# Output projection of a hybrid decoder layer: six of eight pairs of token tiles by seven block products instead of eight

## The chip, the cores and the metric

The kernel runs on one core of a Trainium2 chip. The metric is the device time of one execution in microseconds (us). Before the change the median of three runs is 2264.36 us (2264.03 to 2264.9).

The core's engines run at the same time, each through its own list of instructions in order: TensorE (PE) for matmuls and transposes, VectorE (DVE), ScalarE (ACT) and GpSimd (POOL) for element-wise work, and SyncE (SP), which issues nearly all DMAs. An instruction waits on semaphores for what it needs; everything behind it on the same engine waits with it.

## The reference

One layer of a causal decoder over 2048 tokens of width 1024, in float32:

```python
nx = rmsnorm(h, attn_norm_g[l])
proj = jnp.einsum('bsd,dp->bsp', nx, w_in[l])
...
mixed = jnp.concatenate([o_a, o_b], axis=-1).astype(h.dtype)
h = h + jnp.einsum('bsm,md->bsd', mixed, w_out[l])

nm = rmsnorm(h, mlp_norm_g[l])
a = jnp.square(jax.nn.relu(jnp.einsum('bsd,df->bsf', nm, w_ff1[l])))
h = h + jnp.einsum('bsf,fd->bsd', a, w_ff2[l])
return rmsnorm(h, final_norm_g)
```

`o_a` is chunked gated linear attention, `o_b` dilated sliding-window attention. The change concerns the line with `w_out`, and what lies directly around it: the norm behind it and the start of the MLP's first product. `w_out` is 1024 x 1024, `w_ff1` is 1024 x 4096.

## The kernel before

**Precision.** A float32 product is made of three TensorE matmuls in the type fp32r. Each operand is split into a high part (a copy on ACT that rounds, L486) and a low part (the difference, on DVE, L487). `mm3` (L142 to L144) then issues high x high, low x high and high x low into the same PSUM bank.

**Stages.** The input projection comes first; then attention, in units that go through PE, DVE, ACT and POOL, until about 870 us; then the output projection (870 to 1070); then the MLP's first product, and its second.

**The output projection** is the loop at L1399 over 16 token tiles of 128 rows, in the order 0, 4, 1, 5, 2, 6, 3, 7, 8, 12, ... so that tile t and tile t + 4 follow each other. For one tile `mix_T` (L1262) loads 128 rows of the mixed heads (`mixD`, 512 KB) and of the input `x` (512 KB) into one tile `mx`, makes 8 transposes (L510) into two PSUM banks and splits them into `mT`. Then 2 halves of the output width x 8 chunks of the inner size x 3 = 48 matmuls go into two banks of tag "a"; `w_out` lies in eight tiles `wo`, loaded and split by `load_wo` (L1088) during the end of attention. DVE adds each bank to the row of x (L1416), and the row is stored to `hD`.

**The norm** of a tile is `norm_to_T` (L1225), one tile later: ACT squares the row with a sum (L181), ACT makes 1/sqrt by Ln and Exp (L175, L176), DVE multiplies the row out of place (L183), PE makes 8 transposes, ACT copies the two banks into the four 128x512 parts of the tile `bb` (L1232): two parts from tile t, two from t + 4. After the second tile DVE forms four sums (L1236 to L1239), one in `bb` and three in a tile `tb`, and seven transposed "token sums" are stored to `hTD` (L1241). These are the token-side operands of the MLP's seven products.

**The MLP's first product** works the same way as the change: 2 x 2 blocks, seven products j in the order 1, 2, 6, 5, 7, 3, 4 instead of eight. `product1` (L1339) issues one product (12 matmuls) and chains it in PSUM; `prep1` (L1289) makes the weight sums of a product two jobs ahead into `w1comb`; `load_w1` (L1281) loads raw weights; `reload` (L1245) loads one token sum from `hTD` into a tile `rb` (1 MB) and splits it into a pair of tiles `hb` in two steps of 128x1024. For the first half of the tokens, three of the seven reloads are issued at the tiles in RELOAD (positions 10, 11, 12), three ahead of the MLP's loop, which begins at L1576, and one in it; `load_w1(0)` and the first two `prep1` are at positions 12 and 13.

**Room.** SBUF tiles come from one pool "u" of 25 places; a new tile waits until the tile that had its place is done with. PSUM has 8 banks: 2 of tag "a", 3 of "c", 2 of "d", 1 of "o".

**Order.** The program is written in the order of the loops, and a scheduler then settles each engine's own order by its estimate of when things are ready; only what is pinned with `keep_in_program_order` stays as written.

Of the kernel before, what the change touches and what calls it, by code (L numbers as in the profile page):

```python
# [18 lines left out]
D = 1024  # L19
# [10 lines left out]
W1AT = 12  # L30
# [4 lines left out]
RELOAD = (10, 11, 12)  # L35
# [81 lines left out]
def emit(tc, a, stop=99):  # L117
# [968 lines left out]
    WO = []  # L1086

    def load_wo(n):  # L1088
        for c in range(len(WO), len(WO) + n):
            raw = slot("woraw")[:, :D]  # L1090
            w = view(slot("wo", FR), (2, D))
            SP.dma_start(raw, wo[:, c])
            A.activation(w[:, 0], raw, AF.Copy)
            V.tensor_tensor(w[:, 1], raw, w[:, 0].bitcast(F32), op=OP.subtract)
            WO.append(w)

# [124 lines left out]
    gM = slot("gs")[:, :D]  # L1221
    bb, tb = slot("bb"), slot("tb")
    rb, TF, TB = [slot("rb")], {}, {}

    def norm_to_T(src, dst, t):  # L1225

        normed(src, dst, gM)
        half, i = t // HT, t % 4
        b = [view(bb[:, 512 * q:], (4, 128)) for q in range(4)]
        k = t % HT // 4  # L1230
        for q, pv in enumerate(transposed(dst)):
            A.activation(b[2 * k + q], pv, AF.Copy)  # L1232
        if k == 0:
            return
        (b11, b21, b12, b22), (t2, t4, t3) = b, [view(tb[:, 512 * q:], (4, 128)) for q in range(3)]
        V.tensor_tensor(b12, b12, b11, op=OP.subtract)  # L1236
# [8 lines left out]
    def reload(j, half, t=None):  # L1245

        if t is None:
            t = rb[turns[0] % len(rb)]
            turns[0] += 1
        SP.dma_start(t[:, :2048], hTD[half, j - 1].rearrange("p c s -> p (c s)"))  # L1250

        def rest():
            if j not in TF:
                TF[j] = [slot(f"hb{j}", FR) for _ in range(2)]
                TB[j] = [view(v, (4, 512)) for v in TF[j]]
            for cs in (slice(0, 1024), slice(1024, 2048)):
                split(*[v[:, cs] for v in TF[j]], t[:, cs])
                yield

        return rest()  # L1260

    def mix_T(t):  # L1262
        u = view(slot("mx"), (2, D))
        to = D - 128 if t < 8 else D
        for cs in (slice(0, 512), slice(512, to)) if t in (0, 4) else (slice(0, to),):
            SP.dma_start(u[:, 0, cs], mixD[t * 128:t * 128 + 128, cs])
        if t not in tiles[:2]:
            SP.dma_start(u[:, 1], x2[t * 128:t * 128 + 128])
        m = view(slot("mT", FR), (2, CH, 128))
        for q, pv in enumerate(transposed(u[:, 0], outs[3, 0][:, t, 1:129] if t < 8 else None)):  # L1270
            split(*[m[:, i, 4 * q:4 * q + 4] for i in range(2)], pv)
        return u, m


# [119 lines left out]

    tiles = [8 * half + i + 4 * k for half in range(2) for i in range(4) for k in range(2)]
    nxt = mix_T(tiles[0])
    late = None
    back = []
    for at, t in enumerate(tiles):  # L1399
        u, m = nxt  # L1400
        if at + 1 < NT:
            nxt = mix_T(tiles[at + 1])
# [7 lines left out]
        for q in range(parts_):  # L1410
            for n in range(2):
# [3 lines left out]
                if q == parts_ - 1:  # L1415
                    V.tensor_tensor(h[:, cs], p[n], u[:, 1, cs], op=OP.add)  # L1416
# [288 lines left out]
```

## Time and profile before

| | |
|---|---|
| median of three runs | 2264.36 us |
| the profiled execution, its own time | 2268.81 us |
| its span on the core | 2266.9 us |
| mean granted TensorE clock | 0.995 |
| output projection, first to last of its matmuls | 869.8 to 1070 us |

The profiled execution is a single one, taken with the profiler on, and a little longer than the median of the runs; differences are formed against its own time.

How to read the lines: the page's first part has, for each engine, the busy time, its share of the span and the number of instructions. PEld is the load of weights into the array, which overlaps with PE. A line of a group is: source line, engine, operation, output tile <- input tiles, shapes, count, then busy time, mean ns of one, and the idle time of the engine just before these instructions with what ended it ("<-DVE pt L882": DVE's result `pt` of line 882). A timeline line is: start, duration, the same names, and in brackets the idle time before. A line of a DMA is: tiles, queue, kind, count, size, and the median us from issue to landing. `ps_a` and so on are PSUM banks by tag.

### The profile page before, as it was taken

Reading aid. Unit: us, or ns where it says so; the run is one execution under the profiler, and the core shown is the slowest. Engines: PE = TensorE matmul, PEld = TensorE weight load, DVE = VectorE, ACT = ScalarE, POOL = GpSimd, SP = SyncE. Lnnn points to the kernel's source line nnn. Section 1 sums busy time; section 2 is a strip of 40 time slices with the busy share of each in tenths; the row PEclk is TensorE's granted clock in tenths of the full one; section 3 lists DMA queues with packets and bytes.
Section 4 is the critical chain, followed back from the end, with each engine's and each line's share of the span. In section 5 each row is a group of like instructions: output and inputs, shape, how many; then the busy total and the mean of one; then the engine's idle time right before and its main releaser. Section 6 shows DMA issues by size and latency. Waiting matters only on the chain.

```text
span 2266.9 us, 35208 instructions
## 1 busy us (share of the span) xinstructions
PE 2239.0 (99%) x12508; PEld 1937.2 (85%) x12508; DVE 1635.2 (72%) x3092; ACT 1216.7 (54%) x2421; POOL 484.8 (21%) x455
## 2 busy tenths in 40 slices
PE   9999999999999999999999999999999999999998
PEld 8977998799999998888888887888888888888876
DVE  8787778766677686445877678767686696566768
ACT  6664446535777883324655557555555433333435
POOL 1210002015286673000000000000006322032462
PEclk9999999999999999999999999999999999999999
DMA  6457854776667973678645456454479997676775
GB/s 205 133 181 226 254 165 124 222 248 224 211 211 218 298 219 130 211 229 281 203 133 160 128 165 220 159 171 156 137 248 286 300 318 264 219 252 240 255 264 177
DMA packets 361440, 478.59 MB, mean 211 GB/s; under 512 B 19957, under 2 KB 269318, under 8 KB 350128
## 3 DMA queue, kind: packets, MB, share of 16 engines
q1 hardware_dynamic: 356766, 467.69, 63.3%
q0 software_dynamic: 4352, 8.39, 2.0%
q8 instruction: 98, 1.61, 0.3%
q14 instruction: 78, 0.64, 0.1%
q10 hardware_dynamic: 146, 0.27, 0.0%
HBM read 326.54 MB, written 154.44 MB: 212 GB/s over the span
## 4 chain that ended last, share of the span: by engine, by line
PE 90%; DVE 3%; issue 2%; DMA 2%; POOL 1%; ACT 1%; POOLq 0%; SPq 0%; ACTq 0%; DVEq 0%
PE ps_a L143 10%; PE ps_a L142 10%; PE ps_a L144 10%; PE ps_c L143 8%; PE ps_c L142 8%; PE ps_c L144 8%; PE ps_a L892 4%; PE ps_d L143 4%; PE ps_d L142 4%; PE ps_d L144 4%; PE ps_o L144 4%; PE ps_o L142 4%; PE ps_o L143 4%; PE ps_d L873 3%; PE ps_c L855 2%
## 5 line engine op out<-in xcount | busy, mean ns | idle before, releaser
L1499 POOL TENSOR_TENSOR bs<-bs,rb 128x1024 f32<-128x1024 f32 x60 | 182.2, 3045 | 1071.1 <-DMA actD<-ring 831.5
L486 ACT ACTIVATE cb<-bs 128x1024 fp32r<-128x1024 f32 x104 | 110.3, 1060 | 275.4 <-issue 127.5
L487 DVE TENSOR_TENSOR cb<-bs,cb 128x1024 fp32r<-128x1024 f32 x104 | 156.4, 1504 | 133.4 <-ACT cb L486 133.3
L487 DVE TENSOR_TENSOR w1comb<-w1raw,w1comb 128x512 fp32r<-128x512 f32 x224 | 153.4, 687 | 89.5 <-ACT w1comb L486 88.9
L864 ACT ACTIVATE pe<-pe,O 128x256 f32<-128x256 f32 (+1 forms) x384 | 158.0, 454 | 54.2 <-DVE O L863 51.8
L892 PE MATMUL ps_a<-v,pt 128*128 128x65 f32 x1200 | 180.2, 255 | 5.3 <-DVE pt L882 4.3
L892 PEld LDWEIGHTS ps_a<-v,pt 128*128 128x128 f32 x1200 | 175.2, 196 | 7.7 <-DVE pt L882 5.4
L486 ACT ACTIVATE w1comb<-w1raw 128x512 fp32r<-128x512 f32 x224 | 139.4, 626 | 76.6 <-PE ps_c L144 27.1
L873 PE MATMUL ps_d<-ident,pe 128*128 128x128 f32 x600 | 159.9, 282 | 0.0
L863 DVE CUSTOM_DVE_ANT_0 pe<-ps_c,nb 128x256 f32<-128x256 f32 (+1 forms) x384 | 126.7, 361 | 43.2 <-PE ps_d L873 16.8
L286 ACT ACTIVATE wcomb<-wraw 128x512 fp32r<-128x512 f32 (+2 forms) x119 | 90.0, 757 | 101.3 <-PE ps_a L143 35.2
L142 PE MATMUL ps_c<-hb,w1comb 128*128 128x512 f32 x336 | 130.8, 389 | 0.5 <-ACT xs L1370 0.5
L143 PE MATMUL ps_c<-hb,w1comb 128*128 128x512 f32 x336 | 130.7, 389 | 0.0
L487 DVE TENSOR_TENSOR ca<-ra,ca 128x1024 fp32r<-128x1024 f32 x84 | 123.8, 1475 | 9.5 <-ACT ca L486 9.5
L144 PE MATMUL ps_c<-hb,w1comb 128*128 128x512 f32 x336 | 130.5, 389 | 0.0
L144 PE MATMUL ps_c<-cb,ca 128*128 128x512 f32 x312 | 121.8, 391 | 0.0
L143 PE MATMUL ps_c<-cb,ca 128*128 128x512 f32 x312 | 121.7, 390 | 0.0
L142 PE MATMUL ps_c<-cb,ca 128*128 128x512 f32 x312 | 121.6, 390 | 0.0
L873 PEld LDWEIGHTS ps_d<-ident,pe 128*128 128x128 f32 x600 | 110.0, 188 | 0.5 <-ACT pe L864 0.2
L1361 ACT ACTIVATE acc<-acc 128x512 f32<-128x512 f32 x96 | 60.7, 632 | 90.5 <-DVE acc L1376 36.2
L351 POOL TENSOR_TENSOR acc<-acc,misc 128x264 f32<-128x264 f32 (+1 forms) x32 | 38.7, 1221 | 316.3 <-DMA wraw<-w_in 204.0
L142 PE MATMUL ps_a<-wo,mT 128*128 128x512 f32 x256 | 101.2, 395 | 0.0
(411 smaller groups left out, 7104.9 us busy)
## 6 DMA issues: line engine op xcount, KB each, us to landing
ra<-actD SPq DMA_DIRECT2D x52, 1024.0 KB, 7.6
actD<-ring SPq DMA_DIRECT2D x176, 256.0 KB, 2.8
rb<-w_ff SPq DMA_DIRECT2D x88, 512.0 KB, 7.1
bs<-w_ff SPq DMA_DIRECT2D x72, 512.0 KB, 5.3
w1raw<-w_ff SPq DMA_DIRECT2D x64, 512.0 KB, 4.2
k<-kD SPq DMA_DIRECT2D x16, 1024.0 KB, 7.7
wraw<-w_in SPq DMA_DIRECT2D x48, 256.0 KB, 3.3
cmb<-boD SPq DMA_DIRECT2D x16, 528.0 KB, 6.5
```

The source lines that it names most:

```text
L142: T.matmul(out, sh, mh, start=first, stop=False, **kw)
L143: T.matmul(out, sl, mh, start=False, stop=False, **kw)
L144: T.matmul(out, sh, ml, start=False, stop=last, **kw)
L286: A.activation(hi, src, AF.Copy, scale=sc)
L486: A.activation(hi, src, AF.Copy)
L487: V.tensor_tensor(lo, src, hi.bitcast(F32), op=OP.subtract)
L863: V.tensor_tensor_reduce(p, s, bias, scale=1.0, scalar=BIG, op0=OP.add, op1=OP.min, accum_out=nm)
L864: A.activation(p, p, AF.Exp, bias=nm, scale=-1.0)
L873: T.transpose(pb[:, i * 128:i * 128 + 128], src, ident)
L892: T.matmul(self.b.opsum[:, n % 4], self.pt[:, i * 128:i * 128 + 128], self.b.v[:, blk, cols], start=first, stop=last)
L1361: A.activation(v, v, AF.Relu)
L1499: (engines or ((G,), (V, V))[len(sums) - 1])[e].tensor_tensor(v, v, r, op=OP.add if op == "+" else OP.subtract)
```

## The change

**Block products.** A pair of token tiles (t, t + 4) is a matrix of 256 x 1024. Split into 2 x 2 blocks (a11, a12 of tile t, a21, a22 of tile t + 4; each 128 x 512) and with `w_out` in 2 x 2 blocks of 512 x 512, its product takes seven block products instead of eight, with sums of blocks on both sides. The pairs 0 and 1 are computed as before, 48 matmuls a tile. The pairs 2 to 7 take seven products of 4 chunks x 3 matmuls. Products 1, 2 and 5 open a bank ("a", "o", "d"); 6, 7 and 4 continue in the bank of product 1, and 3 in that of product 5. After each product DVE adds the bank as it then is to the quarter of the rows that needs it.

```diff
+    def product0(g):
+        p, j = g // 7, order[g % 7]
+        if j in (1, 2, 5):
+            held0[j] = ps({1: "a", 2: "o", 5: "d"}[j])
+        b = held0[{6: 1, 7: 1, 4: 1, 3: 5}.get(j, j)]
+        c = combs0[g % 6]
+        for k in range(4):
+            mm3(b, c[:, 0, k], c[:, 1, k], *wo_part(j, k), k == 0 and j in (1, 2, 5), k == 3, skip_group_check=True)
+        e, n = {1: (0, 0), 2: (0, 0), 6: (0, 1), 3: (0, 1), 5: (1, 1), 7: (1, 1), 4: (1, 0)}[j]
+        x = xhs[p][:, e, 512 * n:512 * n + 512]
+        V.tensor_tensor(x, b, x, op=OP.add)
+        if j in (3, 4):
+            row_done(p, j == 4)
```

**Token blocks.** `raw_block` copies a bank of four transposes into a tile `ar` on ACT (four per pair). `prep0` splits the block of a product, three products ahead, into one of six halves of `mcomb`, and forms four sums in place in `ar` on DVE.

```diff
+    def raw_block(p, e, q):
+
+        if p < 8:
+            if not raw0:
+                raw0.append(view(slot("ar"), (4, 4, 128)))
+            A.activation(raw0[0][:, 2 * e + q], mix_block(p, e, q, "c"), AF.Copy)
...
+        a11, a12, a21, a22 = [raw0[0][:, n] for n in range(4)]
+        j, c = order[g % 7], combs0[g % 6]
+        split(c[:, 0], c[:, 1], {1: a11, 2: a12, 6: a11, 5: a21, 7: a11, 3: a12, 4: a22}[j])
+        if j == 2:
+            V.tensor_tensor(a21, a21, a22, op=OP.add)
+            V.tensor_tensor(a11, a21, a11, op=OP.subtract)
+            V.tensor_tensor(a12, a12, a11, op=OP.subtract)
+        if j == 6:
+            V.tensor_tensor(a11, a22, a11, op=OP.subtract)
```

**Weights.** `load_wo` splits the upper four chunks of `w_out` in two pieces of 128x512 each, which lie in tiles `wb1`, `wb12`. `mix_wo(c)`, called once in each of the four plain tiles, loads two chunks again, forms four sums on POOL and splits them into `wb5`, `wb6`, `wb4`, `wb7`.

```diff
+    def mix_wo(c):
+
+        raw = slot("wtraw")
+        SP.dma_start(raw[:, :D], wo[:, c])
+        SP.dma_start(raw[:, D:2 * D], wo[:, c + 4])
+        b11, b12, b21, b22 = [raw[:, 512 * k:512 * k + 512] for k in range(4)]
+        for dst, x, y, j in ((b12, b12, b11, 5), (b22, b22, b12, 6), (b21, b21, b22, 4), (b11, b22, b11, 7)):
+            G.tensor_tensor(dst, x, y, op=OP.subtract)
+            split(*block_view(j, c), dst)
```

**The norm** is cut into `norm_row` and `norm_sums`, which stand in a list and are taken by `next_norm` after products 0, 1 and 5 of a pair (for the last pair in the MLP's loop). The row is multiplied in place, in the tile `xh` from which it is stored; the four sums are made in place in `bb`, from which the token sums are stored; `tb` is gone. All norm transposes use the banks of tag "c".

```diff
+        V.scalar_tensor_tensor(h, h, r, gM, op0=OP.mult, op1=OP.mult)
...
+        store_T(t, *(((1, 0), (2, 1)) if k == 0 else ((3, 3),)))
+
+    def norm_sums(t):
+
+        b11, b21, b12, b22 = hb4
         V.tensor_tensor(b12, b12, b11, op=OP.subtract)
-        V.tensor_tensor(t2, b22, b12, op=OP.subtract)
-        V.tensor_tensor(t4, b21, t2, op=OP.subtract)
-        V.tensor_tensor(t3, t2, b11, op=OP.subtract)
-        for j, v in ((1, b11), (2, b21), (5, b12), (6, t2), (3, b22), (4, t4), (7, t3)):
-            SP.dma_start(hTD[half, j - 1][:, :, i * 128:i * 128 + 128], v)
+        V.tensor_tensor(b22, b22, b12, op=OP.subtract)
+        V.tensor_tensor(b21, b21, b22, op=OP.subtract)
+        V.tensor_tensor(b11, b22, b11, op=OP.subtract)
+        store_T(t, (5, 2), (6, 3), (4, 1), (7, 0))
```

**The reload** of the first half's token sums takes the form that the second half's had: 14 pieces of 512 KB through two tiles `rb`, loaded from ten products before the MLP on and split in the last six products and the first ones of the MLP. A sum's tiles `hb` take the places of block weights that are done with.

```diff
+    def token_pieces(half, first):
+
+        parts_at = {}
+        for n in range(14):
+            parts_at.setdefault(first + 1 + n * 4 // 5, []).append(n)
...
+        def step(at):
+            if at == first - 3:
+                while len(rb) < 2:
+                    rb.append(slot("rb"))
+                for n in range(4):
+                    load(n)
+            for n in parts_at.get(at, ()):
...
+                split(*[v[:, cs] for v in TF[j]], piece(n))
+                load(n + 4)
```

**The loop** over the products of pairs 2 to 7 (`half0` is `token_pieces(0, -7)`):

```diff
+    for g in range(14, 56):
+        p, i = divmod(g, 7)
+        prep0(g + 3)
+        product0(g)
+        if i in (0, 1, 5):
+            next_norm()
+        if i == 2:
+            load_x(p + 1)
+            raw_block(p + 1, 0, 0)
+            raw_block(p + 1, 1, 0)
+        if i == 3:
+            raw_block(p + 1, 0, 1)
+        if i == 4:
+            raw_block(p + 1, 1, 1)
+            load_mix(p + 2)
+        half0(g - 56)
+        if g == 49:
             load_w1(0)
-        if at == W1AT + 1:
-            prep1(0)
-            prep1(1)
-        late = (h, u[:, 0], t)
+        if g >= 54:
+            prep1(g - 54)
```

More of the change, by code (lines that the diff above doesn't have):

```diff
@@ L29 @@
 SLOT = 2112
-W1AT = 12
 AHEAD, LAG = 3, 2
@@ L1243, in emit @@
-    turns = [0]
[L1245 to L1272, printed above, removed]
+    gs, bb = slot("gs"), slot("bb")
@@ L1393, in some_sums @@
                 sums1.pop(0)
[L1395 to L1402, printed above, removed]
+    order = (1, 2, 6, 5, 7, 3, 4)
+    combs0, raw0, held0 = [], [], {}
+    def raw_block(p, e, q):
+        if p < 8:
+            if not raw0:
+                raw0.append(view(slot("ar"), (4, 4, 128)))
+            A.activation(raw0[0][:, 2 * e + q], mix_block(p, e, q, "c"), AF.Copy)
@@ L1571, in mm2 @@
             n % 4 == 3 and c == 1, skip_group_check=True)
[L1573 to L1574 removed]
     load_w1(1)
[L1576 to L1582 removed]
+    for at in range(len(jobs1)):
         prep1(at + 2)
```

179 lines of the change are left out of this document (119 added, 60 removed).

## The prediction

> **What bounds the kernel now.** I read the page from its top: busy time by engine, then the chain that ended last.
>
> ```profile
> span 2266.9 us, 35208 instructions
> ...
> PE 2239.0 (99%) x12508; PEld 1937.2 (85%) x12508; DVE 1635.2 (72%) x3092; ACT 1216.7 (54%) x2421; POOL 484.8 (21%) x455
> ...
> PE 90%; DVE 3%; issue 2%; DMA 2%; POOL 1%; ACT 1%; POOLq 0%; SPq 0%; ACTq 0%; DVEq 0%
> ```
>
> TensorE is busy 99% of the span and is 90% of the chain. That is an average, so I next read the busy time by engine in the stretches around the output projection (columns: stretch, length, busy time and records of PE, PEld, DVE, ACT, POOL, granted clock, DMA share, GB/s).
>
> ```profile
> 860.00:870.00 10.00, 7.72 (x53) 7.72 (x54) 8.97 (x30) 4.95 (x14) 4.68 (x10) 0.66 0.35 120
> 870.00:920.00 50.00, 50.00 (x251) 41.88 (x250) 25.66 (x46) 11.13 (x26) 6.88 (x9) 1.00 0.42 137
> 920.00:1020.00 100.00, 100.00 (x505) 84.49 (x504) 42.86 (x58) 29.97 (x66) 0.00 (x0) 1.00 0.68 211
> 1020.00:1070.00 50.00, 50.00 (x251) 42.15 (x250) 29.37 (x38) 21.05 (x40) 0.00 (x0) 1.00 0.82 271
> 1070.00:1100.00 30.00, 30.00 (x141) 24.76 (x140) 25.16 (x38) 20.95 (x36) 0.00 (x0) 1.00 0.93 297
> ```
>
> From 870 to 1100 us PE has no idle time at full clock, while DVE is busy 43 to 59% up to 1070 and POOL is nearly free. There, a matmul removed is worth its whole issue interval, as long as what replaces it stays under PE's time. At 1070 to 1100 DVE is at 25.16 of 30: that hand-over to the MLP has little cover left, and 870 was preceded by a stall.
>
> **What is removed, and its price.** Groups of 920 to 1020, one row of the tile `wo` over the whole run, and a stretch of the MLP's matmuls alone:
>
> ```profile
> L142 PE MATMUL ps_a<-wo,mT 128*128 128x512 f32 x127 | 50.2, 395 | 0.0
> ...
> L510 PE MATMUL ps_d<-ident,mx 128*128 128x128 f32 x61 | 9.3, 273 | 0.0
> L510 PE MATMUL ps_c<-ident,mx 128*128 128x128 f32 x60 | 9.0, 272 | 0.0
> ...
> L181 ACT ACTIVATE mx<-mx 128x1024 f32<-128x1024 f32 x8 | 8.4, 1052 | 0.0
> ...
> L486 ACT ACTIVATE mT<-ps_c 128x512 fp32r<-128x512 f32 x8 | 4.8, 599 | 2.6 <-PE ps_c L510 2.6
> ...
> L486 ACT ACTIVATE hb<-rb 128x1024 fp32r<-128x1024 f32 x2 | 2.0, 1065 | 0.0
> ...
> L510 PE MATMUL ps_d<-ident,O 128*128 128x128 f32 x3 | 0.8, 273 | 0.0
> ...
> L142 PE MATMUL ps_a<-wo,mT x256: 387/389/487, 869.8 to 1069.7; 128*128 128x512 f32 x128
> ...
> 1150.00:1175.00 25.00, 25.00 (x112) 1.00 0.49 157
> ```
>
> A record lasts some 390 ns but matmuls overlap, so the price is the interval: 25.00/112 = 0.2232 us. Check: 3 x 127 such matmuls are 85.0 us of the 100, and the 61 + 60 + 3 transposes share the other 15, 0.12 us each. L142 has 256 records, a third of the projection's 768 matmuls. The new kernel keeps four tiles at 48 (192) and gives each of six pairs 7 products x 4 chunks x 3 = 84 where there were 96: 192 + 504 = 696. The 256 transposes stay. So 72 x 0.2232 = **16.1 us off PE**. This term is the surest: the new matmuls have the form of the old.
>
> **What is added off PE.** Prices for a 128x512 on DVE and a 128x1024 split, from the timeline of DVE in its densest stretch, and DVE's multiply for the norm:
>
> ```profile
> 1081.24 2.35 DVE L487 TENSOR_TENSOR hb<-rt,hb 128x1024 fp32r<-128x1024 f32 x2
> ...
> 1085.78 0.68 DVE L487 TENSOR_TENSOR w1comb<-w1raw,w1comb 128x512 fp32r<-128x512 f32 x1
> ...
> 1092.39 0.69 DVE L487 TENSOR_TENSOR w1comb<-w1raw,w1comb 128x512 fp32r<-128x512 f32 x1
> ...
> L183 DVE SCALAR_TENSOR_TENSOR mx<-mx,stats,gs 128x1024 f32<-128x1024 f32 x8 | 10.2, 1277 | 2.2 <-ACT stats L176 2.2
> ```
>
> Between the last two rows lie eleven steps, 6.61 us: 0.60 us each; a 1024-wide split is 1.15, the multiply 1.2. Per pair DVE has 7 adds, 7 splits, 4 token sums, 4 norm sums (22 x 0.60) and 2 multiplies: 15.6 us, against PE's 84 x 0.2232 + 32 x 0.12 = 22.6. So in the steady stage DVE is covered, with 7 us over. ACT's 4 raw copies, 7 splits and 4 transposed copies at 0.6 and 2 squares at 1.05 are 11.1. The block weights of the products are made during the four plain tiles: 16 subtracts of 1.29 on POOL, which has almost nothing to do from 870 on, and 16 x 0.6 us of splits on ACT and on DVE, which have 39 and 24 us free in the first 50; their eight loads of 512 KB meet a DMA share of 0.42. The work itself costs nothing then, hidden under PE's matmuls; were that cover gone, DVE's 24 more adds, 24 sums and 16 splits would cost 38 us. What can cost is order, in four places.
>
> *Attention's tail (before 870).* The eight weight splits become eight of 128x512 and four of 128x1024, in another order. What they cost there now:
>
> ```profile
> 858.03 0.28 PE L873 MATMUL ps_d<-ident,pe 128*128 128x128 f32 x1
> 862.28 0.69 PE L892 MATMUL ps_a<-v,pt 128*128 128x65 f32 x2 [3.97 <-DVE pt L882]
> ...
> 862.98 0.52 PE L892 MATMUL ps_a<-v,pt 128*128 128x65 f32 x2
> ...
> 867.43 0.33 PE L892 MATMUL ps_a<-v,pt 128*128 128x65 f32 x2
> ...
> L1094 DVE TENSOR_TENSOR wo<-woraw,wo x8: 1225/1626/2355, 811.0 to 856.1; 128x1024 fp32r<-128x1024 f32 x8
> L952 POOL TENSOR_TENSOR O<-O,cmb x28: 1273/1294/2269, 636.9 to 876.0; 128x512 f32<-128x512 f32 x28
> ```
>
> DVE's last split, started at 856.1, took part in making PE wait 3.97 us. The new order could remove this stall or make a second: -4 to +4 us. I take 0, since as many bytes are split in the same stretch.
> After that stall the same L892 pair lasted 0.52 us until about 867, and 0.33 from 867.43, so about 2.4 us more went to a slower PE. The Trainium skill, "TensorE: Matmul & The Clock Gate", Part 1, says that an idle window of about 3.4 us halves PE's clock; the trace agrees (3.97 us idle, granted clock 0.66 in that slice). By it a single stall of 3.4 us at the hand-over would cost 2.4 more and the sum would be 2258; by the row taken stall by stall, each below that length, nothing is added. The sum below uses the latter.
>
> *From plain tiles to products (about 920).* `mix_wo(3)` loads 2 x 512 KB through SP, then 4 POOL subtracts (1.29 each) and 4 splits. In the issue order, its load stands on SP behind the `hTD` stores of the second tile's norm, and ACT's raw copies for the third pair stand behind its third split.
>
> ```profile
> 900.48 0.69 DVE L1416 TENSOR_TENSOR mx<-ps_a,mx 128x512 f32<-128x512 f32 x1 [2.07 <-PE ps_a L144]
> ...
> 907.89 0.69 DVE L1236 TENSOR_TENSOR bb<-bb 128x512 f32<-128x512 f32 x1 [0.38 <-ACT bb L1232]
> ...
> 913.20 0.69 DVE L1416 TENSOR_TENSOR mx<-ps_a,mx 128x512 f32<-128x512 f32 x1 [0.69 <-PE ps_a L144]
> ...
> hD<-mx SPq DMA_DIRECT2D x16, 512.0 KB, 3.3
> hTD<-bb SPq DMA_DIRECT2D x32, 256.0 KB, 3.7
> mx<-x SPq DMA_DIRECT2D x13, 512.0 KB, 6.3
> hTD<-tb SPq DMA_DIRECT2D x24, 256.0 KB, 6.3
> ...
> rb<-hTD SPq DMA_DIRECT2D x4, 512.0 KB, 5.9
> ```
>
> A tile takes 12.7 us (900.48 to 913.20, the same add one tile on); four end at 869.8 + 50.8 = 920.6. The norm's copies are done by 907.9; a 512 KB load lands 6.3 later, about 914; three subtracts and a split end at 918.5; four raw copies at 0.6 and the first split on ACT and DVE end at 922.1 or so. PE waits about 2 us for it: **2**, bounds 0 (copies placed earlier) and 6 (one more landing).
>
> *Within the six pairs.* Two waits are new. The norm now multiplies in place, so it waits for the row's store (3.3 us); and `norm_sums` overwrites the tiles from which `hTD` is stored, with `tb` gone, so DVE's second subtract waits for a store that is issued only after ACT's copy: 3.7 to 6.3 us. Behind it on DVE stand bank adds and splits. Splits are made three products ahead (8 us), but a chained bank must be added to `xh` before PE writes it again, one product (12 matmuls, 2.7 us) later. The sums mostly stand where an add has just been done, and DVE has 7 us over per pair. Bounds 0 and 6 (1.2 for each of five hand-overs); I take **1.75**.
>
> *Into the MLP (about 1040 to 1085).* The first product's token sums are 14 splits of 128x1024. Before, their loads were spread from the eleventh tile on; now they start ten products before the MLP, and each sum waits for the weights whose place it takes. `load_w1(0)` is moved behind the last pair's first product, the last pair's norms into the MLP's loop, so DVE has them all in one stretch. I counted in the issue order from the end of the last pair's first product. PE has 133 matmuls and 24 transposes up to the MLP's product 3: 29.7 + 2.9 = 32.6 us. DVE must first issue 12 splits, 2 multiplies and 29 of 128x512: 13.8 + 2.4 + 17.4 = 33.6. Eight entries on, the last row's multiply is through at 40.1, and its transposes are PE's next after 24 more matmuls, at 38.0. So DVE is 1.0 and then 2.1 us behind, if it starts on time; it stands behind a wait for a store then, for which I take half of a row's 3.3 us. The two lags on one engine aren't added: 2.1 + 1.65 = **3.75**, bounds 1 (starts on time, one row hidden) and 8 (one load's 5.9 us in the open beside the 2.1).
>
> **Sum.** -16.1 + 0 + 2 + 1.75 + 3.75 = -8.6. The profiled execution took 2268.81 us (its span 2266.9 and 1.9 around it): 2260.2 for its like. The median of the runs, 2264.36, is 4.45 lower, so the forecast is 2255.8, say **2256**.
>
> **Rivals.**
> (a) *All of it hidden*: stalls under 4 us in all. For: DVE at 43% in 920 to 1020, 7 us over per pair. Against: 25.16 of 30 at the hand-over. About 2.5 us of stalls: 2250.8.
> (b) *Given back at the hand-overs*: all upper halves, 4 + 4 + 6.5 plus 1.6 before 870: 16.1 of stalls, 2264.4, no change. For: the DMA share of 0.82 and 0.93 from 1020 to 1100, which lengthens loads. Against: PE was busy without a gap from 1020 to 1100, with the same splits inside.
> (c) *Slower: a serial reload.* With two `rb` tiles, loads of pieces 5 to 14 wait for a split on DVE; then 5.9 us landing, 1.06 ACT, 1.15 DVE: 8.1 us round. If SP's queue (behind stores that wait for DVE) lets only one product's pieces be in flight, each of the last five sums costs 8.1 rather than a product's 2.7: 27 us, -16.1 + 27 = +10.9, with nothing else, 2275.3. It decides (over 0.2% slower) from 16.1 + 4.5 = 20.6 us, that is 6.8 us per sum. Against it: four pieces are in flight by construction, 4.05 us per sum, which costs 6.7.
> (d) *The change doesn't do what it says*: counts would show 768 matmuls; the code leaves no doubt, so no chance is given.
>
> **Chances.** 0.2% (4.5 us) is about what can be told from no change here. Forecast (stalls of 4 to 11.5 us, 2252 to 2260) 0.44; (a) 0.18; (b) 0.22; (c) 0.16. So faster 0.62, same 0.22, slower 0.16. Range 2248 (no stall, 2248.3) to 2268, which leaves out most of (c); the forecast's own range is 2252 to 2260.
>
> **What would show it.** In the changed profile: 232 records of each third of the projection's matmuls; PE idle of some 2 us near 920 put down to a split or a raw copy, small gaps put down to bank adds of `xh` in between, and 3 to 4 us just before and in the MLP's first round put down to `hb` or to the norm's multiply; DVE nearly full there. Wrong would be: a gap over 3.4 us followed by half clock, `hb` splits idle on `rb` loads each round (then c), or no gaps (then a).

## The result and the profile after

The changed kernel takes 2281.51 us (median of four runs, 2278.43 to 2283.72) where the kernel before takes 2264.63 on the same chip (four runs, 2264.03 to 2266.3). The ratio is 1.0072 with an interval of 1.0055 to 1.009: slower by 0.7%, where 2256 was forecast and the range ended at 2268. The profiled execution took 2281.68 us, 12.87 more than the one before.

The first lines of the page of the changed kernel: span, busy time by engine, and shares of the chain that ended last.

```profile
span 2279.8 us, 35292 instructions
...
PE 2231.8 (98%) x12436; PEld 1928.3 (85%) x12436; DVE 1694.4 (74%) x3172; ACT 1250.1 (55%) x2483; POOL 502.2 (22%) x471
...
PE 85%; DMA 5%; DVE 4%; issue 3%; ACT 2%; POOL 1%; SPq 0%; POOLq 0%; DVEq 0%; ACTq 0%
```

PE has 72 records fewer (12436 for 12508), as counted, but only 7.2 us less busy time where 72 x 0.2232 = 16.1 were to go; and its idle time (span less busy) rose from 27.9 to 48.0. To see where, the busy time of the changed kernel by stretches (columns as before: length, PE, PEld, DVE, ACT, POOL, granted clock, DMA share, GB/s): first the whole stretch from attention's end to the MLP, then the stretches that were shown of the kernel before, then every ten microseconds in which the clock was below 0.99.

```profile
780.00:1124.00 344.00, 318.13 (x1847) 274.68 (x1847) 262.12 (x529) 195.94 (x440) 92.21 (x116) 0.96 0.69 223
...
860.00:870.00 10.00, 9.96 (x70) 9.36 (x70) 9.30 (x30) 6.33 (x20) 5.12 (x11) 0.84 0.99 375
870.00:920.00 50.00, 46.02 (x214) 37.94 (x213) 35.82 (x48) 15.93 (x33) 24.18 (x20) 0.93 0.49 165
920.00:1020.00 100.00, 93.77 (x478) 78.23 (x477) 73.01 (x103) 48.90 (x97) 6.57 (x5) 0.97 0.68 214
1020.00:1070.00 50.00, 45.34 (x216) 36.60 (x216) 39.29 (x55) 29.18 (x53) 0.00 (x0) 1.00 0.73 227
1070.00:1100.00 30.00, 24.44 (x111) 19.61 (x110) 24.31 (x32) 17.59 (x31) 0.00 (x0) 0.89 0.86 271
...
820.00:830.00 10.00, 7.71 (x63) 7.31 (x62) 5.69 (x14) 5.96 (x16) 9.63 (x13) 0.96 0.84 255
830.00:840.00 10.00, 10.00 (x82) 9.78 (x82) 9.61 (x34) 8.57 (x26) 9.17 (x9) 0.87 0.38 144
880.00:890.00 10.00, 6.02 (x17) 4.45 (x16) 9.90 (x19) 3.01 (x6) 1.97 (x2) 0.69 0.18 47
890.00:900.00 10.00, 10.00 (x48) 8.27 (x47) 5.92 (x6) 3.07 (x8) 6.43 (x4) 0.97 0.43 138
920.00:930.00 10.00, 5.75 (x35) 4.61 (x33) 10.00 (x10) 3.50 (x6) 6.57 (x5) 0.91 0.22 63
930.00:940.00 10.00, 8.02 (x33) 6.65 (x34) 7.21 (x12) 7.34 (x15) 0.00 (x0) 0.75 0.75 223
1080.00:1090.00 10.00, 5.41 (x28) 4.21 (x27) 10.00 (x13) 4.96 (x7) 0.00 (x0) 0.93 0.76 217
1090.00:1100.00 10.00, 9.03 (x34) 7.03 (x35) 6.24 (x9) 6.36 (x14) 0.00 (x0) 0.73 0.83 251
```

The row of the same stretch before (its MLP stands 10 us earlier, so it ends at 1114):

```profile
780.00:1114.00 334.00, 328.06 (x1934) 285.93 (x1933) 206.53 (x453) 161.20 (x384) 70.88 (x100) 0.99 0.68 217
```

Beside the rows that the prediction shows, PE has lost 4.0 us from 870 to 920, 6.2 to 1020, 4.7 to 1070 and 5.6 to 1100, where it had lost none, and DVE is at 73 rather than 43 us in the hundred from 920 and full in 920 to 930 and 1080 to 1090.

So most of the 12.9 us arises between 780 and the MLP. Matched matmul by matmul, the changed kernel is even 1.5 us ahead shortly before 780 (PE's row L1052 of 776.27 before, now L1050, starts at 774.80), and 10.2 us behind in the MLP (the 5000th matmul from the end starts at 1114.9 before and at 1125.1 after): the stretch loses 11.7. It has 19.9 us more of idle time (25.9 for 5.9) and 9.9 less of busy time, of which 1.5 are matmuls of attention that had run before 780. So of the 16.1 us of matmuls that went only 8.4 show: the others took 7.7 longer, and the low clock of the slices agrees: with 860 to 870, (1 - clock) x 10 us adds up to 13.5 us, before the change to 3.4 (860 to 870 alone, at 0.66). Some of that fell where PE had nothing to do. The other 2.7 us appear far into the MLP; they were not followed.

The idle time is found in PE's timeline: all waits over 0.3 us from 780 to 1124 (start, duration, names, in brackets the wait and what ended it).

```profile
828.26 1.19 PE L890 MATMUL ps_a<-v,pt 128*128 128x65 f32 x8 [2.29 <-ACT pt L878]
...
858.95 0.44 PE L890 MATMUL ps_a<-v,pt 128*128 128x65 f32 x2 [3.10 <-ACT pt L878]
...
885.04 0.80 PE L140 MATMUL ps_a<-wb,mT 128*128 128x512 f32 x1 [3.98 <-DVE xh L1541]
...
926.83 0.55 PE L1336 MATMUL ps_c<-ident,mx 128*128 128x128 f32 x3 [2.22 <-ACT ar L1467]
...
931.98 1.12 PE L1266 MATMUL ps_c<-ident,xh 128*128 128x128 f32 x4 [4.01 <-ACT ar L1467]
...
1055.88 0.50 PE L141 MATMUL ps_d<-wb,mcomb 128*128 128x512 f32 x1 [1.72 <-DVE mcomb L485]
...
1062.52 0.47 PE L140 MATMUL ps_d<-wo,mcomb 128*128 128x512 f32 x1 [1.34 <-ACT stats L173]
...
1067.22 0.50 PE L140 MATMUL ps_a<-hb,w1comb 128*128 128x512 f32 x1 [1.49 <-ACT w1comb L484]
...
1090.76 0.80 PE L140 MATMUL ps_a<-hb,w1comb 128*128 128x512 f32 x1 [5.36 <-ACT xs L1434]
```

Nine waits, 25.5 us, in four places: attention's tail (5.4; before it was 5.0, of which 3.97 at 862.28), one at 885 in the plain tiles, which no step of the prediction had (4.0), the hand-over to the products (6.2) and the one to the MLP (9.9). Between 932 and 1055 there is none: the six pairs run as they should. Each place was followed back to its cause.

**885: POOL beside DVE.** PE waits for DVE's add of the bank, L1541, which starts at 884.31. What DVE and POOL did just before, and again around 920, each from its own timeline:

```profile
878.05 1.32 DVE L936 TENSOR_TENSOR gla<-gla,cmb 128x8 f32<-128x8 f32 x1
...
884.31 0.68 DVE L1541 TENSOR_TENSOR xh<-ps_a,xh 128x512 f32<-128x512 f32 x1
...
921.05 1.77 DVE L485 TENSOR_TENSOR wb<-wtraw,wb 128x512 fp32r<-128x512 f32 x1
922.74 1.77 DVE L1274 TENSOR_TENSOR bb<-bb 128x512 f32<-128x512 f32 x1
...
926.09 0.68 DVE L1541 TENSOR_TENSOR xh<-ps_a,xh 128x512 f32<-128x512 f32 x1
```

```profile
878.05 3.92 POOL L1118 TENSOR_TENSOR wtraw<-wtraw 128x512 f32<-128x512 f32 x3
...
913.99 6.06 POOL L1118 TENSOR_TENSOR wtraw<-wtraw 128x512 f32<-128x512 f32 x4 [14.32 <-DMA wtraw<-w_out]
920.62 6.68 POOL L1118 TENSOR_TENSOR wtraw<-wtraw 128x512 f32<-128x512 f32 x4 [0.58 <-DMA wtraw<-w_out]
```

While POOL subtracts, a DVE operation of eight elements per partition takes 1.32 us, as long as one of POOL's (3.92/3 = 1.31), and one of 512 takes 1.77 rather than 0.68, in step with POOL's 6.68/4 = 1.67. The eight-element ones come in a chain that ends attention, which takes 4.9 us here (877.14 to 882.02); the one of 879.41 took 0.17, in the gap between two of POOL's. The bank's add stands behind this chain, and behind three multiplies of attention (L948, 1.8 us). The add at 926.09, which reads one operand from PSUM, takes its usual 0.68 although POOL is still at work.

**927 and 932: late weights.** The last two groups of subtracts wait for their loads, 14.32 us in the first case. SyncE's timeline shows where the loads stood:

```profile
889.22 13.15 SPq L1488 DMA_DIRECT2D hD<-xh  x2
...
907.01 0.53 SPq L1114 DMA_DIRECT2D wtraw<-w_out  x1
...
914.75 0.60 SPq L1114 DMA_DIRECT2D wtraw<-w_out  x1
```

The queue stood from 889 to 902 at the row's store, which waits for DVE's last add of the tile; so the loads left at 907 and 914.75, the slowed subtracts ended only at 927.3, and ACT, which takes each split in order, reached the raw copies that PE waits for (L1467) at 926.19. The wait at 932 ends with the third of these copies: on ACT it stands behind the squares of a norm, and those wait for DVE's add of 929.58.

**1056 to 1091: DVE full.** DVE's timeline before the first of these waits and inside, then ACT's around the last:

```profile
1047.46 0.69 DVE L1274 TENSOR_TENSOR bb<-bb 128x512 f32<-128x512 f32 x1 [2.78 <-DMA hTD<-bb]
...
1058.16 0.68 DVE L1508 TENSOR_TENSOR xh<-ps_a,xh 128x512 f32<-128x512 f32 x1
```

```profile
1089.16 1.06 ACT L484 ACTIVATE hb<-rb 128x1024 fp32r<-128x1024 f32 x1 [2.41 <-DMA rb<-hTD]
1090.13 0.58 ACT L1434 ACTIVATE xs<-ps_a 128x512 f32<-128x512 f32 x1
```

DVE waits 2.78 us for the store of a token sum before it may overwrite it, and from 1047.5 to 1074 it isn't idle once. PE's last wait ends with ACT's copy of an MLP bank, which stands behind a split that waited 2.41 for its reload. That load was issued only at 1083.25, when DVE's split of 1082.01 had freed its place: a late DVE and a reload's round trip act together here.

### The profile page after: what moved, and what is told of

Read it like the earlier page. It is cut to its first block, busy times and chain, and to the rows that moved or that the text cites. A ratio compares the mean times of both kernels' runs of the same rounds, so it can differ in the third digit from the quotient of the medians.

```text
span 2279.8 us, 35292 instructions
## 1 busy us (share of the span) xinstructions
PE 2231.8 (98%) x12436; PEld 1928.3 (85%) x12436; DVE 1694.4 (74%) x3172; ACT 1250.1 (55%) x2483; POOL 502.2 (22%) x471
## 4 chain that ended last, share of the span: by engine, by line
PE 85%; DMA 5%; DVE 4%; issue 3%; ACT 2%; POOL 1%; SPq 0%; POOLq 0%; DVEq 0%; ACTq 0%
PE ps_a L141 8%; PE ps_a L140 8%; PE ps_a L142 8%; PE ps_c L141 8%; PE ps_c L142 8%; PE ps_c L140 8%; PE ps_a L890 4%; PE ps_d L141 4%; PE ps_d L140 4%; PE ps_d L142 4%; PE ps_o L142 4%; PE ps_o L141 4%; PE ps_o L140 4%; PE ps_d L871 3%; PE ps_c L853 2%
## 5 line engine op out<-in xcount | busy, mean ns | idle before, releaser
L485 DVE TENSOR_TENSOR cb<-bs,cb 128x1024 fp32r<-128x1024 f32 x104 | 162.5, 1563 | 137.3 <-ACT cb L484 137.2
L485 DVE TENSOR_TENSOR ca<-ra,ca 128x1024 fp32r<-128x1024 f32 x84 | 118.6, 1412 | 5.8 <-ACT ca L484 5.8
L142 PE MATMUL ps_a<-wcomb,tb 128*128 128x256 f32 (+1 forms) x344 | 97.7, 284 | 0.0
```

Source lines behind the costliest of these rows:

```text
L142: T.matmul(out, sh, ml, start=False, stop=last, **kw)
L485: V.tensor_tensor(lo, src, hi.bitcast(F32), op=OP.subtract)
```

## The experiments

Each kernel was timed against the kernel before on the same chip. In the last column: PE's waits over 0.3 us from 780 to 1130 us in its profiled execution.

| run | edit of the changed kernel | matmuls off | median us | ratio [interval] | PE's waits, us |
|---|---|---|---|---|---|
| (the kernel before) | - | 0 | 2264.63 | 1 | 5.4 |
| (the change) | none | 72 | 2281.51 | 1.0072 [1.0055, 1.009] | 25.5 |
| e1_sums_dve | weight sums on DVE | 72 | 2270.56 | 1.0012 [1.0002, 1.0022] | 17.3 |
| e2_last_plain | last pair plain | 60 | 2275.35 | 1.0038 [1.0026, 1.005] | 21.6 |
| e3_three_plain | three plain pairs ahead | 60 | 2275.77 | 1.0035 [1.0022, 1.0048] | 17.8 |
| e4_plain_both | e2 and e3 | 48 | 2271.04 | 1.0011 [1.0, 1.0022] | 16.4 |
| e5_last_plain_dve | e1, last pair plain, loads sooner | 60 | 2268.48 | 1.0003 [0.999, 1.0016] | 14.5 |
| e6_raw_early | e1, first raw copies sooner | 72 | 2265.24 | 0.9986 [0.9971, 1.0] | 14.6 |
| e7_fewer_sums | e1, eight token sums left out | 72 | 2271.71 | 1.002 [1.0005, 1.0035] | 18.8 |
| e8_all_three | e5 and e6 | 60 | 2270.24 | 1.0009 [0.9997, 1.0022] | 15.5 |
| f1_own_place | e6, token sums without the wait for stores | 72 | 2265.9 | 1.0 [0.9989, 1.0011] | 15.6 |
| f2_norm_apart | e6, norm out of place | 72 | 2276.84 | 1.0044 [1.003, 1.0057] | 21.3 |
| f3_raws_sooner | e6, each pair's raw copies a product sooner | 72 | 2265.23 | 0.9986 [0.9977, 0.9996] | 10.7 |
| f4_both | f1 and f3 | 72 | 2268.56 | 1.0004 [0.9996, 1.0013] | 16.0 |
| g1_no_low_halves | e6, 14 low halves left out | 72 | 2261.09 | 0.9975 [0.9965, 0.9984] | 10.7 |
| g2_raws_pool | raw copies sooner, sums on POOL | 72 | 2281.67 | 1.0065 [1.0047, 1.0083] | 20.0 |

### Weight sums on DVE (e1)

```diff
-            G.tensor_tensor(dst, x, y, op=OP.subtract)
+            V.tensor_tensor(dst, x, y, op=OP.subtract)
```

> The sixteen weight sums of mix_wo go from POOL to DVE, nothing else. Theory P (POOL's subtracts slow DVE where both run): the 4.0 us gap of PE at 885 us and the half clock behind it go, DVE's 128x8 operations there are back at about 0.2 us from 1.2, and the hand-over near 925 loses about 3 of its 6.2 us: about 2270 us. Theory Q (the loads of w_out stand on SP behind stores that wait, and ACT's raw copies behind their splits): DVE only gets 16 x 0.6 us more, the gaps at 925 stay near 6 us: 2278 to 2282.

Sixteen subtracts move to the engine that is busier, and the ratio falls by 0.6%, some 13.6 us. The grouped rows of DVE's eight-element operation at that line (ns min/median/max, first and last start): the change, e1, and the same operation before.

```profile
L936 DVE TENSOR_TENSOR gla<-gla,cmb x2: 1159/1242/1325, 878.0 to 879.6; 128x8 f32<-128x8 f32 x2
```

```profile
L936 DVE TENSOR_TENSOR gla<-gla,cmb x2: 160/166/173, 879.0 to 879.4; 128x8 f32<-128x8 f32 x2
```

```profile
L938 DVE TENSOR_TENSOR gla<-gla,cmb x2: 165/168/172, 877.8 to 878.2; 128x8 f32<-128x8 f32 x2
```

With POOL's subtracts gone the operation is back at 0.166 us, and the wait at 885 is gone. At the hand-over to the products 2.23 and 0.34 us of wait are left of 6.2; those into the MLP stay (1.74, 1.34, 1.45, 4.08). That POOL's subtracts slowed DVE is shown by these rows: the chain is through in 1.7 us rather than 4.9. The 13.6 us are the price of the whole edit: 8.2 of waits, and most of the rest clock, as the stretches at half clock between 780 and the MLP go from 27.3 to 17.1 us. A new order is part of it, too: the scheduler now has the bank's add (880.69) ahead of the three multiplies, so the 4.0 us at 885 are not POOL's alone. PE's timeline of e1 at the hand-over:

```profile
922.08 0.55 PE L1336 MATMUL ps_c<-ident,mx 128*128 128x128 f32 x3 [2.23 <-ACT ar L1467]
...
926.34 0.63 PE L142 MATMUL ps_a<-wb,mcomb 128*128 128x512 f32 x1
926.76 0.63 PE L140 MATMUL ps_a<-wb,mcomb 128*128 128x512 f32 x1
...
930.73 0.40 PE L142 MATMUL ps_o<-wo,mcomb 128*128 128x512 f32 x1
930.97 0.40 PE L140 MATMUL ps_o<-wo,mcomb 128*128 128x512 f32 x1
```

After waits of 2.23 and 0.34 us the matmuls start 0.42 us apart, and from about 930.5 on 0.24. The granted clock is 0.50 from 923.54 to 930.37. So half rate also follows a wait well below the 3.97 us of the kernel before.

### The pairs next to the hand-overs made plain (e2, e3, e4)

e2 computes the last pair with 96 matmuls instead of 84, so that its token blocks need no sums close to the MLP; e3 makes pairs 0 to 2 plain and spreads the weight sums over tiles 1 to 4; e4 does both. Weight sums stay on POOL.

```diff
-    for g in range(14, 56):
+    for g in range(14, 49):
...
+    for e in range(2):
+        m = nxt
...
+                mm3(b[n], m[c // 4][:, 0, c % 4], m[c // 4][:, 1, c % 4],
+                    *wo_part(((1, 12), (2, 3))[c // 4][n], c % 4), c == 0, c == CH - 1)
```

```diff
-    for at in range(4):
+    for at in range(6):
...
-        mix_wo(at)
+        for c in {1: [0], 2: [1], 3: [2], 4: [3]}.get(at, ()):
+            mix_wo(c)
...
-    for g in range(14, 56):
+    for g in range(21, 56):
```

> The last pair is computed plainly (12 more matmuls, 2.7 us), five pairs by seven products; its split tiles lie in the places of mcomb. Theory D (DVE is crowded and late where the last pair's products, the 14 reload splits and the MLP's first weights meet, and the reload's round trips follow from it): the gaps of 9.9 us from 1055 to 1091 and some 3 us of slow clock shrink to under 3: about 2271 us. Rival R (the round trip of the reload through two rb tiles sets it, whatever DVE has to do): the gaps stay, 2282 to 2284.

> Three pairs plain at the start (12 more matmuls, 2.7 us), and mix_wo(0) to mix_wo(3) at the second to fifth tile, away from attention's tail. If the stalls at 885 and 925 come from the place of mix_wo (P or Q, both): 6.5 and 9 us go, about 2269 us, with PE idle under 1.5 us between 870 and 960. If the hand-over costs its 6 us wherever it lies, since raw copies and first splits can't be made ahead: the gap stands near 945, and the time is about 2277.

> Both: pairs 0, 1, 2 and 7 plain, four pairs by seven products, 48 matmuls fewer than before (10.7 us). If the three stalls are separate and both changes remove theirs: 2281.5 - 15.5 - 13 + 5.4 = about 2258 us, faster than the kernel before by 0.3%. If the hand-overs keep half of their cost: 2268 to 2272.

In e2 the waits into the MLP fall from 9.9 to 3.8 us (0.41, and 3.38 for a split on ACT, which stood in order behind a reload); the wait at 885 (3.98) and those at the hand-over to the products (3.93, 3.09) stay. In e3 the early waits shrink (0.86 and 0.97 in the plain tiles, 1.24 and 1.76 behind them), and 6.6 us stay before the MLP. Both are some 0.35% better than the change although 12 x 0.2232 = 2.7 us of its gain are given up. Together they come to 1.0011, with 1.75 and 1.93 us the longest waits left behind attention: half of each hand-over's loss remained. Fewer products are no cure; they only thin out the work that is late.

### The order at the first hand-over (e6, g2)

e6 is e1 with the four raw copies of the third pair written ahead of the last weight sums; g2 does this alone and leaves the sums on POOL.

```diff
+        if at == 3:
+            for q, k in ((0, 0), (1, 0), (0, 1), (1, 1)):
+                raw_block(2, k, q)
         mix_wo(at)
...
         if at == 3:
-            for q, e in ((0, 0), (1, 0), (0, 1), (1, 1)):
-                raw_block(2, e, q)
             load_mix(3)
```

> Weight sums on DVE (e1), and the four raw copies of the third pair written ahead of mix_wo(3), six pairs by products. Theory Q (ACT's raw copies are late at the hand-over because they stand behind the splits of weights whose loads come late): the 2.2 us gap near 922 and the slow clock behind it shrink to under 1: 1.000 of the kernel before, 2 to 3 us under e1. Rival: the product's bank adds and first splits on DVE are as late as the copies, and the gap only changes its name: as e1, 1.0012.

> The changed kernel with the raw copies ahead of mix_wo(3), the weight sums left on POOL. If the two causes add up: the gaps of 2.2 and 4.0 us near 926 and 932 go but for about 1 to 2, the 4.0 at 885 stays, and the time is 5 to 9 us under the changed kernel, about 1.004 of the kernel before. If POOL's slowing of DVE alone makes the hand-over late (splits of 1.5 to 1.8 us on DVE): 3 or more of the 6.2 us stay, 1.006 or above.

In e6 the waits at the hand-over are 0.43 and 0.54 us, and the time is 0.9986 of the kernel before. In g2 the copies are as early, but 3.71 us for DVE's late add and 3.01 for a late split of `mcomb` remain, and the time is that of the change, as the second expectation had it. So the order is worth 0.26% (1.0012 to 0.9986) once POOL is out of the way, and 0.07%, inside the intervals, while it isn't: of two causes at one place, one hid the other.

### The last pair once more (e5, e8)

e5 is e1 with the last pair plain, its transposes and the first reloads moved forward; e8 adds e6's order.

```diff
-            if at == first - 3:
+            if at == (-12 if half == 0 else first - 3):
...
-    half0, half1 = token_pieces(0, -7), token_pieces(1, 7 * (NP - 1))
+    half0, half1 = token_pieces(0, -6), token_pieces(1, 7 * (NP - 1))
```

> Weight sums on DVE and the last pair plain, the reload's first loads issued two products earlier, its first splits one later, and the last pair's transposes two products earlier than in e2. If e2's 3.4 us gap at 1050 was ACT waiting in order for a reload that had been issued too late, it goes: PE idle under 2 us from 1040 to 1110; with 60 matmuls fewer than before (13.4 us) and some 5 us of gaps at attention's end and 3 to 4 with slow clock near 922: about 0.997 of the kernel before (2258). If the reload's round trip holds ACT or DVE wherever its loads are put: 1.000 or above.

> e5 with the raw copies of e6: if both hand-overs are mended, 13.4 us of matmuls are saved against PE gaps that exceed the kernel before's by under 3 us: about 0.9955 of its time (2254). If e6's copies don't help: as e5.

In e5's profiled execution 3.9 us of wait are left before the MLP, and its span was 2258.9 us, but that execution was the fastest of ten; by the median there is no gain. e8 did not add the two gains: PE has a wait of 4.97 us at 930.59 for a first split of `mcomb`, as DVE stood in order at a weight load that had not landed (3.48 us). The copies were early, the load was not.

### What the stores' waits are worth (e7, f1, f2)

e7 (on e1) leaves out the eight subtracts of the last two pairs' token sums, among which I took the one that waits to be. f1 (on e6) puts the second sum into a place of its own, so that DVE needn't wait for a store; f2 multiplies the norm out of place.

```diff
-        V.tensor_tensor(b12, b12, b11, op=OP.subtract)
...
+        if t not in (tiles[13], tiles[15]):
+            V.tensor_tensor(b12, b12, b11, op=OP.subtract)
```

```diff
-        V.tensor_tensor(b22, b22, b12, op=OP.subtract)
+        t2 = hb4[4]
+        V.tensor_tensor(t2, b22, b12, op=OP.subtract)
```

```diff
-        V.scalar_tensor_tensor(h, h, r, gM, op0=OP.mult, op1=OP.mult)
+        V.scalar_tensor_tensor(scr, h, r, gM, op0=OP.mult, op1=OP.mult)
```

> Weight sums on DVE (e1); left out are the eight DVE sums of the norms of the last two pairs, so the second half's token sums of these tiles are stored unsummed, with the same stores. It takes 4.8 us from DVE and its wait of 3.0 us for a store just ahead of the hand-over to the MLP. Theory D (DVE's lateness sets the gaps from 1050 to 1084): of 8.6 us at most 3 stay, about 0.9985 of the kernel before, 6 us under e1. Rival R (the reload's round trips set them): the gap of 4.1 us at the end of them stays, at most 2 us under e1.

> On e6. The norm's first sum goes to a place of its own (the half of gs that held the squares; the squares go to the part of bb that this row is about to fill), so DVE no longer waits for the store of the part that it overwrites. Theory S (this wait, 2.8 to 3.0 us of DVE per pair and the last of them just ahead of the hand-over, makes DVE late into the MLP): the waits of DVE on stores of bb go, and of e6's 6.7 us of gaps from 1050 to 1099 under 3 stay: 3 to 4 us under e6. Rival (DVE waits for ACT's late split there, and the store's wait hides in it): gaps and time as e6.

> On e6. The norm multiplies the row into gs instead of in place, so DVE doesn't wait for the store of the row. If that wait (1.2 to 1.9 us each at 1022 and 1062 in e6) costs: PE's gap of 1.4 at 1024 goes, 1 to 3 us under e6. If the new wait (the next row's square... goes to bb, the product into gs only when the transposes before have read it) is as long: as e6.

e7 met neither: the norms lag a pair, so the sum with the wait (2.84 us at 1040.84) belongs to the pair before and was not among those left out; the last wait (4.08 in e1) went, another grew to 3.48, and the time is e1's. f1 answers the question better. DVE's waits by what they were for, 920 to 1110 us (total, times, longest), in e6:

```profile
DVE bb L1274 <- DMA hTD<-bb: 9.3, 5, 2.8
```

In f1 all but 1.3 of these 9.3 us are gone, and yet PE's waits from 1050 to 1100 are 7.2 us for 6.7, all its waits 15.6 for 14.6, and the ratio is 1.0 for 0.9986. The step of the prediction that priced them (within the pairs, and half a store before the MLP) was about a wait that DVE can afford. f2 is worse, with 1.47, 1.69 and 1.96 us of PE's wait for DVE's split at the second product of three pairs, and 13.2 us of the same store waits; why the multiply out of place makes them longer I didn't settle.

### Earlier copies, and less work (f3, f4, g1)

f3 (on e6) makes each next pair's raw copies one product sooner; f4 joins it with f1. g1 (on e6) doesn't compute the 14 low halves of the first half's token sums on DVE, and lets PE read the high halves in their place.

```diff
-        if i == 2:
-            load_x(p + 1)
+        if i == 1:
             raw_block(p + 1, 0, 0)
             raw_block(p + 1, 1, 0)
-        if i == 3:
+        if i == 2:
+            load_x(p + 1)
             raw_block(p + 1, 0, 1)
-        if i == 4:
+        if i == 3:
             raw_block(p + 1, 1, 1)
```

```diff
-                split(*[v[:, cs] for v in TF[j]], piece(n))
+                if half == 0:
+                    A.activation(TF[j][0][:, cs], piece(n), AF.Copy)
+                else:
+                    split(*[v[:, cs] for v in TF[j]], piece(n))
```

> On e6. The next pair's four raw copies are written one product earlier. If ACT's late split (DVE's 3.1 us wait for mcomb ahead of the hand-over in e1) starts the lateness: DVE's wait goes and the gaps from 1050 shrink by 2 to 4 us, 2 to 4 us under e6. If the store's wait stands behind it: DVE waits there instead, time as e6.

> f1 and f3 together. If either wait alone only uncovers the other: this one is 4 to 6 us under e6, about 0.996 of the kernel before, while f1 and f3 are within 1.5 of e6. If DVE's amount of work between 1040 and 1085 sets the gaps: as e6, 0.9986.

> On e6. Left out are DVE's fourteen low halves of the first half's token sums; PE reads the high halves in their place, with as many matmuls, and all loads, ACT's high halves and the order of the rest stay. DVE has 16 us less to do between 1035 and 1085. Theory D (the amount of DVE's work there): of e6's 6.7 us of gaps from 1050 to 1099 at most 2 stay, 0.995 of the kernel before. Rival R (round trips of the reload, ACT's order): 4 or more stay, 0.997 or above.

f3 has the fewest waits of the full kernels (10.7 us) and e6's time; f4 is no better than either. g1 tells what the hand-over hangs on. The busy time of 1050 to 1090 us (length, PE, PEld, DVE, ACT, POOL, clock, DMA) in the change, in e6 and in g1:

```profile
1050.00:1090.00 40.00, 30.85 (x145) 24.58 (x143) 38.07 (x49) 23.74 (x36) 0.00 (x0) 0.98 0.82 258
```

```profile
1050.00:1090.00 40.00, 35.03 (x155) 27.65 (x155) 33.33 (x44) 25.44 (x44) 0.00 (x0) 0.96 0.85 267
```

```profile
1050.00:1090.00 40.00, 39.56 (x186) 32.41 (x185) 24.22 (x37) 27.39 (x47) 0.00 (x0) 1.00 0.88 281
```

With 9 us of DVE's work out of the stretch PE has no wait in it over 0.3 us: DVE's low halves set it. Whether by the amount of work or as a step in each reload's chain, g1 can't tell, since it takes out both. Of e6's waits 2.4 us stay up to 1099, nearer the first expectation (2) than the second (4), but the ratio is the second's. By the ratios the end gains only 2.5 us over e6 (0.9986 to 0.9975, with intervals that overlap); some is given back at once, as DVE then waits 5.35 us for a store (1088.46) and PE 2.39 (1095.03) for the bank behind it. f3 is the full version that beats both kernels, by 0.14% of the one before (0.04 to 0.23%), a thin margin for the best of twelve full variants; e6 has the same ratio, but an interval that reaches 1.

## Why the prediction was wrong

By its own steps, against the 11.7 us that the stretch from 780 to the MLP lost:

| step | predicted | measured |
|---|---|---|
| 72 matmuls less | -16.1 | -16.1 (72 records fewer, steady pairs without a gap) |
| attention's tail | 0 (-4 to +4) | +0.4 (waits of 5.4 for 5.0) |
| the work of the products "costs nothing" | 0 | +4.0 at 885 |
| from plain tiles to products | +2 (0 to 6) | +6.2 |
| within the six pairs | +1.75 (0 to 6) | 0 |
| into the MLP | +3.75 (1 to 8) | +9.9, less 0.5 that was there before |
| clock, "nothing is added" | 0 | +7.7 |
| sum | -8.6 | +11.6 |

The waits are read from PE's timeline; the clock's term is what then remains of PE's busy time.

**The step that failed first is "16 subtracts of 1.29 on POOL, which has almost nothing to do from 870 on".** The prediction concluded that this work "costs nothing". POOL was free, but its work was not: the subtracts held up DVE, at a place where DVE's chain ends attention and PE has one bank left. e1 shows this: 13.6 us by one edit. No rival had it. The row that would have said so was in the trace of before. DVE's timeline there, then POOL's:

```profile
874.70 1.21 DVE L930 TENSOR_TENSOR gla<-gla,cmb 128x8 f32<-128x8 f32 x1
...
877.66 0.17 DVE L936 TENSOR_TENSOR gla<-gla,O 128x8 f32<-128x8 f32 x1 [0.29 <-ACT gla L935]
```

```profile
874.60 2.68 POOL L952 TENSOR_TENSOR O<-O,cmb 128x512 f32<-128x512 f32 x2
```

The same kind of operation takes 1.21 us beside POOL and 0.17 when POOL has ended (or, at 875.94, in the gap between POOL's two). The prediction had even quoted maxima of 2355 and 2269 ns for DVE's and POOL's operations, and used them only for the tail. The Trainium skill, "SBUF — State Buffer", section "SBUF: two separate sides", states that a DVE instruction with two SBUF inputs and a GpSimd instruction that reads SBUF exclude each other: the one that starts first holds the shared ports for all of its length, and the other is blocked. The trace agrees: 1.16 to 1.33 us beside POOL's 1.31, and 0.68 unchanged for the add that has one input in PSUM.

The prediction's price of DVE's extra work (38 us, which entered no sum) was miscounted, too: 18 more adds, not 24, and 18 more splits of tokens that it left out; DVE has 80 records more (3172 for 3092) and 59.2 us more busy time.

**From plain tiles to products** the order was read rightly in kind (copies behind the splits, the load on SP behind stores), but the duration was taken from undisturbed rows: three subtracts and a split were to end at 918.5, where POOL started the last group only at 920.62. The runs found two causes: POOL first, then ACT's order (e6), which shows only when the first is gone (g2).

**Into the MLP** the count was right in kind, DVE as the bound, and its slack was misjudged. "If it starts on time" was the weak clause: the last pair's first add on DVE (1058.16) came some 8 us after its product's last matmul, behind waits for a split and a store, and there was no room in which to recover. Half a store's 3.3 us was no measure for that. Without the waits for stores nothing is gained here (f1); without DVE's low halves the waits of the stretch go (g1). Rival (c), the serial reload, had the sign but not the size: ACT's four waits for reloads come to 5.4 us in all, not 8.1 per sum, though the last of them is a round trip behind a split of DVE's, as the rival describes it.

**The clock.** The prediction added nothing, since each stall was to be shorter than the 3.97 us of the tail. Three were not (3.98, 4.01, 5.36), and shorter ones counted too (e1 at 922). The Trainium skill, "TensorE: Matmul & The Clock Gate", Part 1, puts the lower clock behind an idle window of about 3.4 us; the runs here differ, as the window need not be idle throughout.

In each of the sixteen profiles the starts of the half-clock stretches lie whole multiples of 3.413 us apart (in the changed kernel 829.14, 859.86, 883.75, 928.13 and 1088.55, among others). Divided into slots by this grid, from 870 to 1130 us every slot at full clock in which PE was idle for 1.93 us or more was followed by one at half clock, none below 1.6 was, and in between both occur (in attention, whose matmuls are smaller, 1.19 us was enough once, in e5). So what counts is how much of a wait falls into one slot. The change's wait of 3.10 us before 858.95 has 2.50 of it in one; e6's of 2.65 before 860.02 is cut in two (3.42 - 2.17 and 3.41 - 1.87 us of idle time), and the clock stays full, up to 865 as well. The slot after that wait in the change, then e6's two:

```profile
859.86:863.27 3.41, 3.41 (x21) 3.41 (x20) 3.00 (x8) 3.41 (x12) 2.77 (x2) 0.50 1.02 401
```

```profile
855.19:858.61 3.42, 2.17 (x22) 1.98 (x21) 1.78 (x4) 2.19 (x5) 3.42 (x4) 1.00 1.05 400
858.61:862.02 3.41, 1.87 (x17) 1.64 (x17) 3.41 (x14) 3.38 (x12) 1.90 (x2) 1.00 1.03 407
```

**What was right:** the price and number of matmuls removed, DVE's cover within the pairs, and the places of the two hand-overs. The gain of 8.6 us was one sure term less three that were priced by undisturbed durations alone.

What stays open: the 2.7 us that the MLP behind adds; how the 4.0 us at 885 divide between POOL and DVE's order, and those into the MLP between DVE's amount of work and the reloads; and why runs of one kernel differ by several microseconds. e5's fastest execution had a mean clock of 0.998, the change 0.990. Since the grid of the clock lies differently against the program in each profile, the same wait can cost half a slot or more in one execution and nothing in another; how much of the spread that is, one profile per kernel can't show.

## What to carry to other kernels

An idle engine is not free when it shares something with a full one: before work is put on POOL, look in the trace for the shortest DVE operations that ran beside a POOL operation and price them by that row. Where an engine is the bound only at a hand-over, count its work from the moment at which it really starts, which the queue in front of it decides. When removing a stall's cause brings nothing, another cause may stand at the same place: remove that one and try again.

## What was unexpected of the hardware

A DVE operation on 128x8 with both inputs in SBUF went from 0.166 to 1.242 us (median of two) beside POOL's subtracts, one on 128x512 from 0.68 to 1.77, while one that reads a PSUM bank stayed at 0.68; POOL's own subtract rose from 1.31 to 1.67 us when DVE's operations beside it were of that size. And the granted clock fell after waits of 2.2 to 2.3 us, for slots of 3.413 us on a grid of their own: after 2.29 us at 828.26 it is 0.50 from 829.14 to 832.55, and in e1 matmuls are 0.42 us apart after 2.23 us; but after e6's 2.65 us at 860.02, cut by a slot's edge, it stays at 1.00.
